# Winograd feed-forward kernel: Pool sums queued one product ahead, upper and lower halves of each operand queued apart, rows of odd tiles loaded later

## The chip, the cores and the metric

The kernel runs on one NeuronCore of a Trainium2 chip. Its engines are TensorE (PE in the profile, with its weight loads as PEld), VectorE (DVE), ScalarE (ACT), GpSimd (POOL) and SyncE (SP, which issues the DMAs). Each engine takes its instructions strictly in the order in which the program issued them; semaphores hold an instruction until what it reads is written and what it overwrites has been read. The metric is device time in microseconds of one execution, the median over runs.

## What is computed

One block of a transformer trunk on 1024 tokens of width 1024, all in float32: RMS norm, sliding-window attention with sinks, output projection, residual; then RMS norm, a SwiGLU feed-forward layer with inner width 2816, residual, and a last RMS norm.

```
h = rms_norm(x, norm_mix);  x = x + sliding_window_sink_attention(h, ...)
gu = rms_norm(x, norm_ffn) @ w_gate_up
x = x + (silu(gu[:, :2816]) * gu[:, 2816:]) @ w_down
out = rms_norm(x, final_norm)
```

## The kernel before, in words

**Precision.** Each float32 operand is split into an upper half (`hi`, a rounded copy in fp32r, written by ScalarE) and a lower half (`lo` = source minus upper half). A product is three matmuls: hi x hi, hi x lo, lo x hi. The `lo` of a gate-up weight is written by VectorE; in the down stage the `lo` of an activation is written by GpSimd and that of a weight by VectorE.

**Seven products for eight.** Both feed-forward matrix products are done in Winograd's form of Strassen's scheme: 2 x 2 blocks, seven products numbered 1 to 7. Some operands are sums or differences of blocks. GpSimd makes these ("sums"), and a summed operand can be split only after its sum.

**Gate-up stage** (lines 873 to 1092). 22 groups `g` of 256 columns, even ones gate, odd ones up. From group 2 on every group is seven products in the order 1, 6, 5, 7, 2, 4, 3, of 12 matmuls each. Products 1 and 2 accumulate in one PSUM bank (A), 6 and 7 in B, 5 and 3 in C, 4 alone in D. The second product of a bank may start only when VectorE has read the first: `u(0)` (line 1011) reads B between products 6 and 7, `c("C", 1, 1, 1)` (line 1015) reads C between 5 and 3. The weights are prepared by `prep` (line 888): optional sums (line 901), `hi` (line 921), `lo` (line 925). `prep_more` (line 936) is called ahead of every product and prepares, into nine slots, the operand for the product eight ahead as soon as the slot of the product just done is free (two operands in one call where slots come in pairs). After each odd group `act_sums` (line 979) makes four sums of the finished activations on GpSimd (line 989) and stores them to DRAM.

**Down stage** (lines 1137 to 1362). Four rounds of 2, 2, 2 and 3 pairs; per round seven products in the order 1, 2, 6, 7, 5, 3, 4; a product is four token columns `j` of 3 matmuls per pair (24 matmuls for 2 pairs, 36 for 3). Its operands sit in 16 slots: per product and pair one of activations ("s", loaded from DRAM) and one of down weights ("w"). `d_steps` (line 1178) gives the steps of an operand: for a weight operand of product 6 two sums (lines 1212 and 1216), of products 7 and 4 one sum (line 1212), then `hi` (line 1232) and `lo` (line 1235). Results leave PSUM at once: in round 0 products 1 and 7 are copied to `y1`, `y7` by ScalarE (line 1314), all others are added to `acc` by VectorE (line 1316). Products 1 and 2 share a bank per column, and so do 6 and 7, and 5 and 3: the second one's matmuls wait until the first one's result has been read. `acc` starts as the rows of the residual, eight DMAs (line 1279). Last come 16 products of four leftover chunks (line 1390) and the final norm.

**Order.** No scheduler reorders anything. A list `Q` holds steps with due times; every matmul of these stages issues one tick, and a tick issues what is due. So a due time decides only the place of a step in its engine's queue, not when it runs. `d_more` (line 1242) is called ahead of every down product and after the last seven gate-up products. Before the change it and `prep_more` strung the steps of an operand one right behind another:

```
for i, st in enumerate(steps):                                  # prep_more
    Q.put(1 + i * spread // len(steps), st)
for k, st in enumerate(st for steps in todo for st in steps):   # d_more
    Q.put(1 + k * spread // total, st)
```

## Time and profile before

| | |
|---|---|
| time, median of 3 runs | 1066.96 us (1066.46 to 1068.29) |
| the profiled execution's own time | 1066.94 us |
| its span, first to last instruction | 1065.1 us |
| granted TensorE clock, mean over the span | 0.979 of full speed |
| busy: PE, DVE, ACT, POOL | 1007.2, 617.8, 454.6, 573.4 us |

Times in the views are microseconds from the start of the span. In a timeline row the columns are start, duration, engine, line, operation, output <- inputs, count, and in brackets the idle time of the engine ahead of the row with what ended it. A matmul shown as 0.4 us long is pipelined: in these stages one starts every 0.233 us. "L1054" is line 1054.

### The profile page before, as it was taken

What the parts mean: (1) busy time and instruction counts of PE and PEld (TensorE: products, weight loads), DVE (VectorE), ACT (ScalarE), POOL (GpSimd) and SP (SyncE); (2) the same over time, 40 slices, a digit from 0 to 9 for tenths busy, and PEclk for the clock granted to TensorE, in tenths of its full rate; (3) what the DMA queues carried; (4) which work ended last, traced back from release to release, by engine and by line L of the source; (5) the groups of instructions that cost most, each with busy time, mean ns of one, the idle gap of its engine ahead of it and who ended that gap; (6) DMA issues with size and microseconds to landing.
All of it is one profiled execution on the core that took longest, in us unless ns stands there. A gap on an engine that the chain in (4) does not pass through costs nothing. (4 is left out here: it accounts for less than half of the span.)

```text
span 1065.1 us, 13843 instructions
## 1 busy us (share of the span) xinstructions
PE 1007.2 (95%) x4740; PEld 828.8 (78%) x4740; DVE 617.8 (58%) x1070; ACT 454.6 (43%) x955; POOL 573.4 (54%) x557
## 2 busy tenths in 40 slices
PE   7999999999986899999999999999998889898997
PEld 7888888888765698787888777778887768687885
DVE  5421778777975665554454554545543467564774
ACT  5432778777844542331332332322323533333334
POOL 4634655565424555375375374374336676667573
PEclk8999999999988999999999999999999899999999
DMA  8458556564437311342231340331336925242202
GB/s 269 132 131 204 151 144 158 145 195 136 140 99 213 124 60 60 129 148 75 75 129 39 129 145 23 129 128 42 129 119 206 351 94 188 89 139 76 92 40 119
DMA packets 98983, 138.28 MB, mean 130 GB/s; under 512 B 6368, under 2 KB 66784, under 8 KB 98912
## 3 DMA queue, kind: packets, MB, share of 16 engines
q1 hardware_dynamic: 98624, 136.61, 41.1%
q8 instruction: 37, 0.61, 0.2%
q10 hardware_dynamic: 288, 0.79, 0.2%
q14 instruction: 34, 0.28, 0.1%
HBM read 99.89 MB, written 35.39 MB: 127 GB/s over the span
## 5 line engine op out<-in xcount | busy, mean ns | idle before, releaser
L1305 PE MATMUL d<-HH 128*128 128x512 f32 x756 | 179.4, 400 | 17.9 <-DVE y L1316 8.1
L1305 PEld LDWEIGHTS d<-HH 128*128 128x128 f32 x756 | 146.1, 194 | 51.1 <-ACT HH L1232 13.1
L967 POOL TENSOR_TENSOR gate<-gate,up 128x512 f32<-128x512 f32 x33 | 47.2, 1430 | 177.5 <-issue 130.9
L925 DVE TENSOR_TENSOR ws<-sum,ws 128x512 fp32r<-128x512 f32 x88 | 81.2, 932 | 92.8 <-ACT ws L921 92.5
L1054 PE MATMUL gu_A<-HH,ws 128*128 128x512 f32 (+2 forms) x552 | 132.3, 388 | 0.0
L1235 POOL TENSOR_TENSOR HH<-raw_s,HH 128x512 fp32r<-128x512 f32 x63 | 90.8, 1456 | 74.9 <-ACT HH L1232 66.1
L251 PE MATMUL pc<-HH,wc_c 128*128 128x512 f32 x480 | 122.0, 398 | 0.0
L1054 PEld LDWEIGHTS gu_A<-HH,ws 128*128 128x128 f32 x552 | 101.7, 188 | 22.9
L921 ACT ACTIVATE ws<-sum 128x512 fp32r<-128x512 f32 x88 | 54.4, 627 | 141.3 <-POOL sum L901 108.3
L251 PEld LDWEIGHTS pc<-HH,wc_c 128*128 128x128 f32 x480 | 87.3, 188 | 17.9
L496 POOL TENSOR_SCALAR t<-t,st 128x256 f32<-128x256 f32 (+1 forms) x128 | 60.7, 494 | 52.2 <-DVE st L494 36.1
L921 ACT ACTIVATE ws<-raw_g 128x512 fp32r<-128x512 f32 x66 | 40.6, 626 | 100.2 <-issue 41.2
L1235 DVE TENSOR_TENSOR HH<-wd,HH 128x512 fp32r<-128x512 f32 x62 | 51.3, 831 | 50.9 <-ACT HH L1232 50.9
L925 DVE TENSOR_TENSOR ws<-raw_g,ws 128x512 fp32r<-128x512 f32 x66 | 65.5, 1002 | 23.6 <-ACT ws L921 22.9
L483 ACT ACTIVATE t<-t,st 128x256 f32<-128x256 f32 (+1 forms) x128 | 61.9, 485 | 26.6 <-DVE st L475 26.5
L1054 PE MATMUL gu_B<-HH,ws 128*128 128x512 f32 x264 | 67.0, 403 | 6.0 <-DVE u L1011 6.0
L1054 PE MATMUL gu_C<-HT,ws 128*128 128x512 f32 (+2 forms) x288 | 67.6, 382 | 0.6 <-DVE ws L925 0.6
L63 POOL TENSOR_TENSOR wc_c<-raw_c,wc_c 128x1024 fp32r<-128x1024 f32 x20 | 48.0, 2402 | 34.9 <-ACT wc_c L60 34.6
L1054 PE MATMUL gu_D<-HT,ws 128*128 128x512 f32 (+2 forms) x276 | 66.5, 388 | 0.0
L1054 PE MATMUL gu_C<-HH,ws 128*128 128x512 f32 x264 | 65.5, 397 | 0.9 <-DVE gate L1015 0.9
L1054 PE MATMUL gu_B<-HT,ws 128*128 128x512 f32 (+2 forms) x276 | 65.9, 387 | 0.0
L1054 PEld LDWEIGHTS gu_B<-HH,ws 128*128 128x128 f32 x264 | 50.5, 192 | 19.3 <-issue 7.3
(173 smaller groups left out, 1946.1 us busy)
## 6 DMA issues: line engine op xcount, KB each, us to landing
raw_g<-in_ffn_w_gate_up_dram SPq DMA_DIRECT2D x44, 512.0 KB, 4.1
raw_s<-actp SPq DMA_DIRECT2D x27, 512.0 KB, 3.4
wd<-in_ffn_w_down_dram SPq DMA_DIRECT2D x22, 512.0 KB, 4.1
raw_c<-in_swa_w_in_dram SPq DMA_DIRECT2D x20, 512.0 KB, 4.1
actp<-up SPq DMA_DIRECT2D x18, 512.0 KB, 5.4
qs<-qst SPq DMA_DIRECT2D x64, 128.0 KB, 2.5
qt<-qs SPq DMA_DIRECT2D x32, 256.0 KB, 4.4
actp<-gate SPq DMA_DIRECT2D x27, 256.0 KB, 4.5
```

What stands on the lines that cost most here:

```text
L63: lo_eng.tensor_tensor(lo, src, f(hi), ALU.subtract)
L251: nc.tensor.matmul(ps, wc[:, wl, k], hh[:, :, hl, k, :], start=(n == 0), stop=(n == 3 * NK - 1))
L483: nc.scalar.activation(self.tt[:, g, b0:], self.tt[:, g, b0:], AF.Exp, bias=st[:, 0, g : g + 1], scale=-1.0, accum_out=st[:, 3, g : g + 1],)
L496: nc.gpsimd.tensor_scalar(self.tt[:, g, b0:], self.tt[:, g, b0:], st[:, 2, g : g + 1], 0.0, ALU.mult, ALU.add)
L921: nc.scalar.activation(w[:, 0], src(), AF.Copy)
L925: nc.vector.tensor_tensor(w[:, 1], src(), f(w[:, 0]), ALU.subtract)
L967: nc.gpsimd.tensor_tensor(gate[:, s], gate[:, s], ups[kp, f_][:, s], ALU.mult)
L1054: nc.tensor.matmul(v4(ps)[:, j0:j1], w[:, wl, k], moving(i, hl, k, j0, j1), start=(first and part != "l" and n == 0), stop=(n == 11), skip ...
L1235: eng.tensor_tensor(dst[:, 1], v4(src()), f(dst[:, 0]), ALU.subtract)
L1305: nc.tensor.matmul(v4(ps), a_[:, a, j], d_[:, b], start=(first and n == 0), stop=(n == 3 * len(ps_) - 1), skip_group_check=True,)
```

## The change

In `prep_more` the sums of an operand come first, 3 ticks apart, then `hi` some `lag` ticks after the first sum and `lo` another `lag` ticks after `hi`; `lag` is 8, or 3 and 4 in the entry of the stage. The second operand of a call follows half a spread later instead of at the same time. The first call in the main loop comes 12 ticks earlier. `act_sums` spaces its four sums by 11 ticks instead of 5 and stores at tick 48 instead of 30.

In `d_more` the sums of weight operands are given out on their own, up to about one product ahead of the operands whose `hi` is due (`nsum` against `ndop`); an operand's `hi` is given out only in a call after its sum has been issued (`summed`), and its `lo` 10 ticks after its `hi`. `BEHIND` keeps a sum that overwrites a block behind the `lo` that still reads it. Calls after the last gate-up products take 3 operands instead of 2, and the queue is no longer emptied (`Q.flush()`) between the stages.

The `acc` tiles are laid out in the order 0, 2, 4, 6, 1, 3, 5, 7; the even rows are loaded at the start of the down stage, the odd ones at ticks 48, 64, 80 and 96 after it, the row of the final norm at tick 150.

```diff
--- before.py
+++ after.py
@@ -923,6 +923,7 @@
         def lo():
             w = ws[item]
             nc.vector.tensor_tensor(w[:, 1], src(), f(w[:, 0]), ALU.subtract)
+            ready.add(item)
             if i == 7:
                 Raw.done(lk)
             if i == 3:
@@ -930,17 +931,21 @@
 
         return steps + [hi, lo]
 
-    made = set()
+    made, ready = set(), set()
     nprep = 0
 
-    def prep_more(n, spread):
+    def prep_more(n, spread, lag=8):
         nonlocal nprep
+        base = 1
         while n and nprep < len(seq) and ws_free(nprep):
-            steps = prep(seq[nprep])
-            for i, st in enumerate(steps):
-                Q.put(1 + i * spread // len(steps), st)
+            *sums_, hi, lo = prep(seq[nprep])
+            for i, st in enumerate(sums_):
+                Q.put(base + 3 * i, st)
+            Q.put(base + (lag if sums_ else 0), hi)
+            Q.put(base + (lag if sums_ else 0) + lag, lo)
             nprep += 1
             n -= 1
+            base += spread // 2
 
     Q = Queue()
 
@@ -986,7 +991,7 @@
             (u0[:, a], u1[:, a], g0[:, a], ALU.subtract),
             (u1[:, b], g1[:, a], u0[:, a], ALU.subtract),
         )):
-            Q.put(2 + 5 * i, lambda dst=dst, x_=x_, y_=y_, op=op: nc.gpsimd.tensor_tensor(dst, x_, y_, op))
+            Q.put(2 + 11 * i, lambda dst=dst, x_=x_, y_=y_, op=op: nc.gpsimd.tensor_tensor(dst, x_, y_, op))
 
         def store():
             rows_ = actp_dram[kp]
@@ -996,7 +1001,7 @@
             nc.sync.dma_start(rows_[1], u0)
             nc.sync.dma_start(rows_[2], u1)
 
-        Q.put(30, store)
+        Q.put(48, store)
 
     def after(g, i):
 
@@ -1046,6 +1051,7 @@
         first = i not in (2, 7, 3)
         if first and part != "l":
             banks[g, letter] = pool.tile([P, 512], F32, tag=tag, name=f"gu_{g}_{letter}")
+        assert (g, i) in ready, (part, g, i, nprep, Q.now)
         ps, w = banks[g, letter], ws[g, i]
         j0, j1 = {"g": (0, 4), "h": (0, 3), "l": (3, 4)}[part]
         n = 0
@@ -1082,13 +1088,13 @@
                             W.want(j + 3)
                         o_mm(i, 2 * c2 + ci, nh, wt)
                 ob_done = j + 1
-                prep_more(2, 8)
+                prep_more(2, 8, 3)
         wts = [W.get(42), W.get(43)]
         for i in range(2):
             for nh in range(2):
                 for c in (6, 7):
                     o_mm(i, c, nh, wts[nh])
-            prep_more(2, 8)
+            prep_more(2, 8, 3)
         ob_done = 44
 
 
@@ -1239,45 +1245,76 @@
 
         return steps + [hi, lo]
 
-    def d_more(n, spread):
-        nonlocal ndop
-        todo = []
-        while n and ndop < len(dops):
+    nsum, d_ready = 0, set()
+
+    def d_more(n, span):
+
+
+        nonlocal ndop, nsum
+        his, tts = [], []
+        while n and len(his) < n and ndop < len(dops):
             o = ndop
             free = (NG - 1, (1, 7, 2, 3)[o // 4]) in done if o < 16 else dops[o - 16][1:] in d_done
-            steps = d_steps(dops[o]) if free else None
+            steps = d_steps(dops[o]) if free and (dops[o] not in summed or summed[dops[o]]) else None
             if steps is None:
                 break
-            todo.append(steps)
+            his.append((dops[o], steps[-2], steps[-1]))
             ndop += 1
-            n -= 1
-        total = sum(len(st) for st in todo)
-        for k, st in enumerate(st for steps in todo for st in steps):
-            Q.put(1 + k * spread // total, st)
+        while nsum < min(ndop + n + 1, len(dops)):
+            op = dops[nsum]
+            if op in summed:
+                steps = d_steps(op)
+                if steps is None or op[1] in BEHIND and ("w", BEHIND[op[1]], op[2]) not in d_ready:
+                    break
+
+                def last(op=op, st=steps[-3]):
+                    st()
+                    summed[op] = True
+
+                tts += [*steps[:-3], last]
+            nsum += 1
+        for k, st in enumerate(tts):
+            Q.put(2 + k * span // len(tts), st)
+        for k, (op, hi, lo) in enumerate(his):
+
+            def low(op=op, lo=lo):
+                lo()
+                d_ready.add(op)
+
+            Q.put(1 + k * span // len(his), hi)
+            Q.put(11 + k * span // len(his), low)
+
+    BEHIND = {6: 1, 4: 2}
+    summed = {op: False for op in dops if op[0] == "w" and op[1] in (6, 7, 4)}
 
     o_products()
     for n, item in enumerate(head):
-        if Q.now >= 96 + 48:
-            prep_more(2, 11)
+        if Q.now >= 96 + 36:
+            prep_more(2, 11, 4 if n < 8 else 8)
         product(*item)
         if item[0] != "h":
             done.add(item[1:])
             after(*item[1:])
         if len(head) - 1 - n < 7:
             w_more()
-            d_more(2, 10)
-    Q.flush()
+            d_more(3, 11)
     ht_cm.__exit__(None, None, None)
 
 
     accp = ctx.enter_context(tc.tile_pool(name="accp", bufs=1, reuse_waits="tile"))
-    acc = [accp.tile([P, D], F32, name=f"acc_{t}") for t in range(NT)]
+    acc = {t: accp.tile([P, D], F32, name=f"acc_{t}") for t in (0, 2, 4, 6, 1, 3, 5, 7)}
     y1 = [accp.tile([P, 512], F32, name=f"y1_{j}") for j in range(4)]
     y7 = [accp.tile([P, 512], F32, name=f"y7_{j}") for j in range(4)]
     wbc = row("wbc_fin", "wbc")
-    for t in (0, 2, 4, 6, 1, 3, 5, 7):
+
+    def load_acc(t):
         nc.sync.dma_start(acc[t], x2_dram[t])
-    nc.sync.dma_start(wbc, norm_fin.partition_broadcast(P))
+
+    for t in (0, 2, 4, 6):
+        load_acc(t)
+    for t in (1, 3, 5, 7):
+        Q.put(40 + 8 * t, lambda t=t: load_acc(t))
+    Q.put(150, lambda: nc.sync.dma_start(wbc, norm_fin.partition_broadcast(P)))
 
 
     def d_out(i, j):
@@ -1300,6 +1337,7 @@
             ps = dbanks[bank, j]
             n = 0
             for p in ps_:
+                assert {("s", i, p), ("w", i, p)} <= d_ready
                 a_, d_ = d_slot["s", i, p], d_slot["w", i, p]
                 for a, b in ((0, 0), (0, 1), (1, 0)):
                     nc.tensor.matmul(
@@ -1355,7 +1393,7 @@
     for r, ps_ in enumerate(drounds):
         for i in DORDER:
             w_more()
-            d_more(2 * len(ps_) + 1, 12 * len(ps_) - 3)
+            d_more(2 * len(ps_) + 1, 12 * len(ps_))
             d_product(r, i)
             for p in ps_:
                 d_done.add((i, p))
@@ -1372,12 +1410,10 @@
     for j in range(4):
         for k, st in enumerate(y_sums(j)):
             Q.put(6 + 22 * j + 5 * k, st)
-    while ndop < len(dops):
+    while len(d_ready) < len(dops):
         w_more()
-        before = ndop
         d_more(16, 4)
         Q.tick()
-        assert ndop > before
     for t in range(NT):
         for nh in range(2):
             pool, tag = (psg, "g") if nh else (psa, "a")
```

## Rows read from the trace of the kernel before

**Rows 1.** The page, busy time of each engine over the span.
```profile
PE 1007.2 (95%) x4740; PEld 828.8 (78%) x4740; DVE 617.8 (58%) x1070; ACT 454.6 (43%) x955; POOL 573.4 (54%) x557
```

**Rows 2.** The waits of TensorE: waited for, us in total, times, longest.
```profile
PE d L1305 <- DVE y L1316: 8.1, 2, 4.0
PE d L1305 <- ACT y L1314: 6.4, 1, 6.4
PE gu_B L1054 <- DVE u L1011: 6.0, 3, 2.1
...
PE d L1305 <- DVE acc L1316: 3.4, 2, 3.2
```

**Rows 3.** The timeline of TensorE, gate-up stage from group 2 on.
```profile
415.14 2.96 PE L1054 MATMUL gu_A<-HH,ws 128*128 128x512 f32 x12
417.94 2.96 PE L1054 MATMUL gu_B<-HT,ws 128*128 128x512 f32 x12
...
499.35 2.96 PE L1054 MATMUL gu_C<-HT,ws 128*128 128x512 f32 x12
504.40 4.58 PE L1054 MATMUL gu_B<-HH,ws 128*128 128x512 f32 x12 [2.09 <-DVE u L1011]
508.81 2.96 PE L1054 MATMUL gu_A<-HH,ws 128*128 128x512 f32 x12
...
666.52 3.04 PE L1054 MATMUL gu_B<-HH,ws 128*128 128x512 f32 x12 [2.08 <-DVE u L1011]
...
707.83 3.04 PE L1054 MATMUL gu_B<-HH,ws 128*128 128x512 f32 x12 [1.87 <-DVE u L1011]
```

**Rows 4.** The timeline of all engines, group 6 (it starts at 493.75).
```profile
497.62 1.30 POOL L901 TENSOR_TENSOR sum<-raw_g,raw_g 128x512 f32<-128x512 f32 x1
...
499.61 1.11 DVE L925 TENSOR_TENSOR ws<-sum,ws 128x512 fp32r<-128x512 f32 x1 [4.74 <-ACT ws L921]
500.12 1.74 POOL L901 TENSOR_TENSOR sum<-sum,raw_g 128x512 f32<-128x512 f32 x1
...
502.56 1.08 DVE L925 TENSOR_TENSOR ws<-sum,ws 128x512 fp32r<-128x512 f32 x1 [1.85 <-ACT ws L921]
...
503.57 0.68 DVE L1011 TENSOR_TENSOR u<-gu_B,p 128x512 f32<-128x512 f32 x1
```

**Rows 5.** The timeline of TensorE, down stage and the leftover products.
```profile
817.10 5.61 PE L1305 MATMUL d<-HH 128*128 128x512 f32 x24
829.10 23.84 PE L1305 MATMUL d<-HH 128*128 128x512 f32 x96 [6.39 <-ACT y L1314]
...
873.98 39.91 PE L1305 MATMUL d<-HH 128*128 128x512 f32 x168 [4.04 <-DVE y L1316]
917.92 58.98 PE L1305 MATMUL d<-HH 128*128 128x512 f32 x252 [4.03 <-DVE y L1316]
980.12 34.30 PE L1305 MATMUL d<-HH 128*128 128x512 f32 x144 [3.22 <-DVE acc L1316]
1014.25 43.68 PE L1390 MATMUL dl<-HH 128*128 128x512 f32 x192
```

**Rows 6.** The groups by line, 817 to 1014 us: busy, mean ns | idle before, releasers.
```profile
L1235 POOL TENSOR_TENSOR HH<-raw_s,HH 128x512 fp32r<-128x512 f32 x58 | 83.7, 1458 | 53.1 <-ACT HH L1232 44.3 <-PE d L1305 7.4 <-issue 1.3
...
L1235 DVE TENSOR_TENSOR HH<-wd,HH 128x512 fp32r<-128x512 f32 x55 | 45.3, 823 | 43.3 <-ACT HH L1232 43.3
...
L1232 ACT ACTIVATE HH<-wd 128x512 fp32r<-128x512 f32 x58 | 35.8, 622 | 52.6 <-POOL wd L1212 47.6 <-PE d L1305 4.9
```

**Rows 7.** The timeline of all engines around the start of the down stage.
```profile
810.88 1.76 POOL L967 TENSOR_TENSOR gate<-gate,up 128x512 f32<-128x512 f32 x1
...
827.94 0.63 ACT L1232 ACTIVATE HH<-wd 128x512 fp32r<-128x512 f32 x1 [2.97 <-POOL wd L1212]
828.47 0.58 ACT L1314 ACTIVATE y<-d 128x512 f32<-128x512 f32 x1
```

**Rows 8.** The DMA issues, 780 to 880 us: KB each, median us to landing.
```profile
acc<-x2s SPq DMA_DIRECT2D x8, 512.0 KB, 7.3
```

## The prediction

> **What bounds the kernel now.** I read the busy times first: TensorE is busy 95% of the span, the next engine 58% [rows 1]. So a gain can only come from its idle time. Next, its waits: 17.9 us in the down stage (8.1 + 6.4 + 3.4), most of the rest of what this change can reach behind `u` in the gate-up stage [rows 2]. Then its timeline, to put these waits into places and to see what they cost beyond the idle time itself.
>
> Gate-up: a product starts 2.80 us after the one before it (415.14 to 417.94) [rows 3], so a tick is 2.80 / 12 = 0.233 us. From 415.14 to the first down product at 817.10 [rows 3, 5] there are 20 groups of 7 products: 140 x 2.80 = 392.0 us at full pace, 401.96 in the trace, so **9.96 us are lost**. Most of it sits at three like places, where the second product of bank B waits for `u(0)`: 2.09, 2.08 and 1.87 us. The first also costs clock: that product needs 4.41 us (504.40 to 508.81) instead of 2.80 [rows 3].
>
> Down: 756 matmuls at a tick each are 176.4 us; from 817.10 to 1014.25 [rows 5] it takes 197.15. So **20.75 us are lost**: 17.9 of waiting [rows 2], the rest slower matmuls behind the waits (the 96 from 829.10 show 23.84 us instead of 22.4) [rows 5].
>
> Why TensorE waits is read in the other engines. In group 6 VectorE starts a `lo` at 502.56 that has waited 1.85 us for ScalarE's `hi`, which waited for a sum; the sums stand on GpSimd in turns with the four of `act_sums`. Only behind this `lo` comes `u(0)`, at 503.57, though product 6 was through long before, and product 7, due at 499.35 + 2.80 = 502.15, starts at 504.40 [rows 3, 4]. The down stage has the same chain in nearly every weight operand of products 6, 7 and 4: ScalarE idles 47.6 us ahead of `hi` for a sum, VectorE 43.3 us ahead of `lo` for a `hi`, GpSimd 44.3 us ahead of its own `lo` for a `hi` that stands behind the stalled one [rows 6]. The three engines run one after the other, and the result reads that TensorE needs queue behind them. Nobody lacks throughput.
>
> **The change part by part.** No instruction is added or removed; all of it is order. So every term is waiting.
>
> *Gate-up, sums and `act_sums`.* By the new due times, in a group like 6, GpSimd's order is multiplication, first `act_sums` step, first weight sum, second weight sum, and only then the second `act_sums` step (tick 21 instead of 15). Up to the first weight sum this is the old order, so I take its row: done at 498.92. `hi` follows (0.63), then the same `lo` as before, 499.61 to 500.72 [rows 4]. The other operand's `lo` falls due at tick 29, behind `u(0)` at 28. `u(0)` can then run from 500.72 to 501.40, 0.75 us before 502.15: the wait goes. The fourth wait (ahead of product 3, from the same mixing one product later) goes alike: its sum at tick 37 stands ahead of the last `act_sums` step, not behind all four. Everywhere else `lo` is due 8 ticks (1.9 us) behind `hi` and ahead of `u(0)` only where the sum was given out 16 ticks before. What is late next: weight operands are ready 22 ticks after their call at the latest, and are used eight products (96 ticks) after it; the store of `act_sums` moves by 18 ticks (4.2 us), and its tiles are next written 84 ticks (19.6 us) after it; the raw tiles freed by a later `lo` refill two groups ahead. I cost these at nothing. Bounds for the stage: 0 to 9.96 us gained, and a loss as in the third rival; I take 9.96, since the place with the least room keeps 0.75 us.
>
> *Down, sums ahead and `lo` 10 ticks behind `hi`.* Following the due times call by call, each operand's `lo` is issued at least 19 ticks (4.4 us) ahead of the product that reads it (tightest in the last round, product 6 and 7), and each sum a call ahead of its `hi`. GpSimd has 58 `lo` at 1.458 us [rows 6] and by the code 36 sums; at 1.30 [rows 4] that is 84.6 + 46.8 = 131 us of the 176. Its fullest stretch is the start of the last round: 15 steps in 80 ticks (18.7 us), 20.5 us of work, and the `hi` concerned come over 20 ticks after their sums. VectorE then waits for nothing of GpSimd's, and results are read within the 15 ticks (3.5 us) that the order gives them. A raw tile is refilled over 50 ticks (11.7 us) before its `hi`. Bounds: 0 to 20.75 us gained; I take all but the boundary, below.
>
> *Boundary of the stages.* Here ScalarE copies `y` only behind a `hi` that waited 2.97 us for its sum: 6.39 us of TensorE's idle time [rows 5, 7]. In the new order that `hi` (product 7, second pair) stands ahead of the copies too, and its sum is the fifth GpSimd step after the multiplication that ends at 812.64 [rows 7]: two sums, a `lo`, two sums. At 1.30, 1.458 or 1.74 us each [rows 4, 6] it ends at 819.1, 819.9 or 821.3; three `hi` and a copy (2.3 us) [rows 7] later the first `y` is out, at 821.4, 822.2 or 823.6. Product 2 is due at 817.10 + 24 x 0.233 = 822.7. So 0 to 0.9 us are left, and I take 0.5.
>
> *Odd rows later, no flush.* SP now issues four loads, not nine, ahead of the raw tiles. Even rows go out behind a store that needs a multiplication on GpSimd ending near 822.5; with 7.3 us to landing [rows 8] they are there at 829.8, four adds end by 832.5, and product 7 first needs VectorE at 833.9: hidden, by 1.4 us. The last odd tile is loaded at tick 96 and added to at tick 123, 6.3 us later, so VectorE may wait 1 us; product 3 needs that column only 15 ticks (3.5 us) on. Nothing, then; if the loads took 3 us longer, some 2 us would show once.
>
> *Entry* (lags of 3 and 4, first call 12 ticks earlier): one wait under a microsecond may go; counted at nothing.
>
> **Sum**, against the profiled execution's own 1066.94 us (the median is 1066.96, the same): 1066.94 - 9.96 - 20.75 + 0.5 = **1036.7 us**. What lies outside the two stages is untouched.
>
> **A rule that speaks against it.** A sum takes 1.30 us when VectorE is idle and 1.74 beside a `lo`, which itself takes 1.11 [rows 4]. The Trainium skill, GPSIMD Engine Reference, section 1. Specifications, says that GpSimd shares its SBUF interfaces with VectorE and contends with instructions of two SBUF inputs; by that rule, the trace agrees, sums no longer followed by a waiting VectorE would all run at the long time. It is the first rival.
>
> **The rivals.**
> 1. *GpSimd stretched by VectorE.* With every step at 1.74 us [rows 4] the first weight sum of a group like 6 ends 1.3 us later, `u(0)` ends at 502.7 and product 7 loses 0.75 us with the hand-over, three times 0.75 = 2.3; the boundary keeps 0.9 instead of 0.5. In the down stage 94 steps x 1.74 = 164 us, still under 176. Result 1039.4. For: both long and short times are in the trace. Against: VectorE is busy 58% [rows 1], and mean 1.458 [rows 6] already holds much overlap. Chance 0.16.
> 2. *The boundary keeps its wait.* GpSimd still works off the last multiplications and four sums while ScalarE's copies stand behind a `hi`. If something ahead (a late down weight, a `lo`) pushes that chain by 6 us, the old 6.39 us [rows 5] stay: 1036.7 + 5.9 = 1042.6. For: it is the only place where my room is under 1 us and several queues meet. Chance 0.13.
> 3. *`u(0)` is late in every group: slower.* The new order puts a `lo` at ticks 17 to 26 ahead of `u(0)` in all 20 groups. If that `lo` begins to wait beyond about 6.6 us into the group (product 7 is due at 8.40; `lo`, `u(0)` and hand-over need 1.8), every group loses what group 6 lost, 504.40 - 502.15 = 2.25 us [rows 3]: 1036.7 + 45.0 = 1081.7. For: the fixed place in the queue. Against: in the rows the first sum is done 5.2 us into the group even behind two other steps [rows 4]. Chance 0.03.
> 4. *It does not do what it says:* the sums still run late, because GpSimd reaches them no sooner, and the waits move instead of going: 1066 us. Against: GpSimd idles 44.3 us of the down stage for others [rows 6]. Chance 0.03.
> 5. *Only the down stage gains*, because another read takes the place of `u(0)`: 1036.7 + 9.96 = 1046.7. Chance 0.05.
>
> **How the numbers follow.** Forecast 1036.7 with chance 0.60; its own range, the boundary and the entry, is 1035 to 1039. The range takes in rivals 1 and 2: its low end is 1066.94 - 30.71 less about 1 us for the entry and the spread of runs, 1035.0; its high end 1042.6 and the runs' spread of 1.3, 1044.0. It leaves out rivals 3 to 5, 0.11 of the chance, and some room for what I missed. A measurement of this kernel tells about 0.2% (2.1 us) from no change. Faster by more: 0.60 + 0.16 + 0.13 + 0.05 = 0.94; within: 0.03 (rival 4); slower: 0.03 (rival 3).
>
> **What would show it.** Right: TensorE's waits for `u` at line 1011 and for `y` and `acc` at line 1316 are gone; the down stage takes 176 to 178 us and groups 2 to 21 take 392; ScalarE's wait for sums at lines 1212 and 1216 and VectorE's for `hi` fall from over 40 us to a few; the clock stays full through both stages. Wrong: a wait of several us behind the copies to `y` at the start of the down stage (rival 2); `u` waits in many groups (rival 3); mean times of GpSimd's sums near 1.7 with short waits left (rival 1); new waits of TensorE for an operand's `lo`, which would mean that the operands came too late after all.

## The result and the profile after

| | before | changed |
|---|---|---|
| time, median of 4 runs each | 1067.62 us (1066.46 to 1069.64) | 1038.68 us (1037.09 to 1040.88) |
| the profiled execution's own time | 1066.94 us | 1039.65 us |
| its span | 1065.1 us | 1037.9 us |
| granted TensorE clock, mean over the span | 0.979 | 0.983 |

The ratio is 0.973, with a 95% interval of 0.970 to 0.975: 2.7% faster. The forecast was 1036.7 us in a range of 1035 to 1044. The profiled execution of the changed kernel lies 1 us above its median, so the working below is against 1039.65.

The page of the changed kernel, busy time of each engine (it answers to [rows 1]): TensorE's busy time fell by 6.4 us, GpSimd's rose by 15.5 and VectorE's by 25.3 at the same number of instructions.

```profile
PE 1000.8 (96%) x4740; PEld 826.4 (80%) x4740; DVE 643.1 (62%) x1070; ACT 454.8 (44%) x955; POOL 588.9 (57%) x557
```

The waits of TensorE in the changed kernel, from 400 us on (they answer to [rows 2]; waited for, us in total, times, longest). Of some 24 us in [rows 2], 5 are left, and the larger of the two is a wait that the kernel before did not have in this place: `acc`, once, 4.1 us, ahead of product 7 of the first round.

```profile
PE d L1343 <- DVE acc L1354: 4.1, 1, 4.1
PE gu_B L1060 <- DVE u L1016: 0.9, 1, 0.9
```

The timeline of TensorE in the changed kernel (it answers to [rows 3, 5]).

```profile
415.45 2.96 PE L1060 MATMUL gu_A<-HH,ws 128*128 128x512 f32 x12
...
738.51 3.06 PE L1060 MATMUL gu_B<-HH,ws 128*128 128x512 f32 x12 [0.90 <-DVE u L1016]
...
808.62 16.74 PE L1343 MATMUL d<-HH 128*128 128x512 f32 x72
829.42 158.06 PE L1343 MATMUL d<-HH 128*128 128x512 f32 x684 [4.07 <-DVE acc L1354]
987.32 43.70 PE L1426 MATMUL dl<-HH 128*128 128x512 f32 x192
```

Two numbers are read from this view for every kernel below. **A** is the gate-up stage, from the start of group 2 to the first down product: 808.62 - 415.45 = 393.17 us (401.96 before [rows 3, 5]). **B** is the down stage, from its first product to the first leftover product: 987.32 - 808.62 = 178.70 us (197.15 before [rows 5]). They account for the result: 8.79 + 18.45 = 27.24 of the 27.29 us between the two profiled executions. What lies ahead of group 2 differs between kernels that are the same there (its start lies between 412.2 and 415.6 us in all runs), so the whole times of single runs tell little below 2 us, and A and B are compared. A repeats to a few hundredths in kernels with the same gate-up part and no change at its end; B lies between 176.15 and 178.70 us in the five kernels below that have the changed down part as it is (changed, e2, e7, e8, e11), so a difference in B of 2.5 us tells nothing.

The groups by line in the changed kernel, 808.62 to 987.3 us (they answer to [rows 6]): VectorE's idle time ahead of the `lo` of weights went from 43.3 to 5.0 us, ScalarE's for a sum from 47.6 to 2.5. But one GpSimd sum now takes 1584 ns, and one VectorE `lo` 1098 instead of 823.

```profile
L1241 POOL TENSOR_TENSOR HH<-raw_s,HH 128x512 fp32r<-128x512 f32 x60 | 88.0, 1484 | 22.5 <-ACT HH L1238 22.5
L1241 DVE TENSOR_TENSOR HH<-wd,HH 128x512 fp32r<-128x512 f32 x54 | 59.2, 1098 | 5.0 <-ACT HH L1238 5.0
...
L1238 ACT ACTIVATE HH<-wd 128x512 fp32r<-128x512 f32 x58 | 35.5, 619 | 7.8 <-PE d L1343 4.9 <-POOL wd L1218 2.5
L1218 POOL TENSOR_TENSOR wd<-wd 128x512 f32<-128x512 f32 x10 | 15.8, 1584 | 3.4 <-DVE HH L1241 3.4
```

The timeline of all engines in the changed kernel, around the start of the down stage (it answers to [rows 7]). The first copies of `y` run at 813.51 and wait for nothing. What is late is the residual: SP issues the even rows at 815.74, the first add waits for them until 822.46, the add at 827.46 for the last one, and TensorE, which stopped at 829.42 - 4.07 = 825.35, goes on behind the next add. The two single `acc` rows at 825.04 and 827.39 are the first two odd ones.

```profile
813.51 1.55 ACT L1352 ACTIVATE y<-d 128x512 f32<-128x512 f32 x3
814.88 0.33 SPq L978 DMA_DIRECT2D act<-gate  x1
815.74 2.29 SPq L1311 DMA_DIRECT2D acc<-x2s  x4
822.46 0.69 DVE L1354 TENSOR_TENSOR acc<-d,acc 128x512 f32<-128x512 f32 x1 [7.05 <-DMA acc<-x2s]
...
825.04 0.43 SPq L1311 DMA_DIRECT2D acc<-x2s  x1
...
827.39 0.43 SPq L1311 DMA_DIRECT2D acc<-x2s  x1
827.46 0.69 DVE L1354 TENSOR_TENSOR acc<-d,acc 128x512 f32<-128x512 f32 x1 [0.55 <-DMA acc<-x2s]
```

Windows of the changed kernel (us, then PE, PEld, DVE, ACT and POOL busy with their counts, granted clock, DMA share, GB/s). The wait is paid twice: 4.07 us of idling, and then 35 matmuls in 10.58 us at a granted clock of 0.72, while the DMA engines run at their full share.

```profile
825.42:829.42 4.00, 0.00 (x1) 0.00 (x1) 2.65 (x5) 0.26 (x1) 4.00 (x4) 0.88 1.02 408
829.42:840.00 10.58, 10.58 (x35) 8.49 (x36) 4.92 (x8) 5.45 (x10) 3.35 (x4) 0.72 1.03 413
840.00:860.00 20.00, 20.00 (x90) 16.57 (x89) 16.55 (x22) 8.19 (x16) 18.90 (x14) 1.00 0.43 152
```

### The profile page after: what moved, and what is told of

It reads as the page before. It is cut to its first block, busy times and chain, and to the rows that moved or that the text cites. A ratio compares the mean times of both kernels' runs of the same rounds, so it can differ in the third digit from the quotient of the medians.

```text
span 1037.9 us, 13830 instructions
## 1 busy us (share of the span) xinstructions
PE 1000.8 (96%) x4740; PEld 826.4 (80%) x4740; DVE 643.1 (62%) x1070; ACT 454.8 (44%) x955; POOL 588.9 (57%) x557
## 4 chain that ended last, share of the span: by engine, by line
PE 63%; DMA 1%; POOL 1%; DVE 1%; ACT 0%; issue 0%; SPq 0%; POOLq 0%; DVEq 0%; ACTq 0%
PE d L1343 16%; PE gu_A L1060 12%; PE gu_B L1060 12%; PE gu_C L1060 12%; PE gu_D L1060 6%; PE dl L1426 4%; DMA acc<-x2s 1%; PE mo L1073 1%; DVE ws L925 0%; POOL sum L901 0%; POOL wc_oB L63 0%; POOL xr L641 0%; PE pt_b L620 0%; SPq L1311 0%; ACT wc_oB L60 0%
## 5 line engine op out<-in xcount | busy, mean ns | idle before, releaser
L1343 PE MATMUL d<-HH 128*128 128x512 f32 x756 | 174.8, 394 | 4.1 <-DVE acc L1354 4.1
L1343 PEld LDWEIGHTS d<-HH 128*128 128x128 f32 x756 | 143.7, 190 | 35.0 <-DVE acc L1354 4.5
L972 POOL TENSOR_TENSOR gate<-gate,up 128x512 f32<-128x512 f32 x33 | 50.4, 1529 | 162.5 <-issue 71.5
L251 PEld LDWEIGHTS pc<-HH,wc_c 128*128 128x128 f32 x480 | 87.3, 188 | 17.9
L925 DVE TENSOR_TENSOR ws<-raw_g,ws 128x512 fp32r<-128x512 f32 x66 | 71.4, 1090 | 35.7 <-ACT ws L921 35.4
L1238 ACT ACTIVATE HH<-raw_s 128x512 fp32r<-128x512 f32 x63 | 39.4, 625 | 85.0 <-PE d L1343 36.7
L1241 DVE TENSOR_TENSOR HH<-wd,HH 128x512 fp32r<-128x512 f32 x62 | 66.4, 1076 | 12.5 <-ACT HH L1238 12.5
L1354 DVE TENSOR_TENSOR acc<-d,acc 128x512 f32<-128x512 f32 x80 | 54.3, 686 | 31.5 <-PE d L1343 21.1
```

Of the source, the lines that this page charges most:

```text
L251: nc.tensor.matmul(ps, wc[:, wl, k], hh[:, :, hl, k, :], start=(n == 0), stop=(n == 3 * NK - 1))
L925: nc.vector.tensor_tensor(w[:, 1], src(), f(w[:, 0]), ALU.subtract)
L972: nc.gpsimd.tensor_tensor(gate[:, s], gate[:, s], ups[kp, f_][:, s], ALU.mult)
L1241: eng.tensor_tensor(dst[:, 1], v4(src()), f(dst[:, 0]), ALU.subtract)
L1343: nc.tensor.matmul(v4(ps), a_[:, a, j], d_[:, b], start=(first and n == 0), stop=(n == 3 * len(ps_) - 1), skip_group_check=True,)
L1354: nc.vector.tensor_tensor(dst, ps, dst, ALU.add)
```

## The experiments

Three open questions: whether the two stages' gains are separate; which of the new spacings carries each; and what the boundary costs. All twelve kernels against the two of the change, A and B as above (times are of one run, except where a range stands):

| kernel | time, us | A, us | B, us |
|---|---|---|---|
| before | 1066.94 | 401.96 | 197.15 |
| changed | 1039.65 | 393.17 | 178.70 |
| e1_gate_only | 1058.34 | 393.16 | 197.62 |
| e2_down_only | 1046.79 | 400.42 | 178.17 |
| e3_lo_close | 1047.17 | 399.20 | 181.64 |
| e4_sums_inline | 1038.18 | 393.16 | 179.42 |
| e5_act_late | 1039.28 | 393.16 | 179.99 |
| e6_rows_at_once | 1036.71 | 393.17 | 177.60 |
| e7_act_sums_old | 1036.70 | 393.78 | 178.41 |
| e8_prep_old | 1040.32 | 395.38 | 176.15 |
| e9_inline_close | 1067.82 | 399.41 | 200.67 |
| e10_odd_copied | 1031.36 (1030.32 to 1032.91, 5 runs) | 393.14 | 171.62 |
| e11_changed_again | 1038.89 (1037.92 to 1041.83, 4 runs) | 393.17 | 177.55 |
| e12_odd_only | 1039.62 | 393.16 | 178.78 |

The kernel before gave 1064.76 to 1067.93 us beside them.

### Each stage alone

e1 is the kernel before with the new `prep_more` and `act_sums`; e2 is the changed kernel with the old ones.

The edit of e1 is the part of the change's diff above `d_steps`, and the calls of `prep_more` (without the assertions). The edit of e2 takes the same part back, save for the lag in two calls, where it is no longer used; these are lines of it:

```diff
...
-            Q.put(base + (lag if sums_ else 0), hi)
-            Q.put(base + (lag if sums_ else 0) + lag, lo)
+            steps = prep(seq[nprep])
+            for i, st in enumerate(steps):
+                Q.put(1 + i * spread // len(steps), st)
...
-            Q.put(2 + 11 * i, lambda dst=dst, x_=x_, y_=y_, op=op: nc.gpsimd.tensor_tensor(dst, x_, y_, op))
+            Q.put(2 + 5 * i, lambda dst=dst, x_=x_, y_=y_, op=op: nc.gpsimd.tensor_tensor(dst, x_, y_, op))
...
-        Q.put(48, store)
+        Q.put(30, store)
...
-        if Q.now >= 96 + 36:
-            prep_more(2, 11, 4 if n < 8 else 8)
+        if Q.now >= 96 + 48:
+            prep_more(2, 11)
```

> Only the gate-up part of the change (prep_more, act_sums, the earlier first call); the down stage as before. My theory, that each part removes its own waits: groups 2 to 21 take about 393 us instead of 402, the down stage stays at about 197, time about 1058. Rival, that TensorE only arrives earlier at the down stage and gives the gain back there waiting for sums or DMAs: the down stage grows to 203 or more, time 1064 or more.

> Only the down part (sums ahead, lo 10 ticks behind hi, odd rows later, no flush); prep_more and act_sums as before. My theory: groups 2 to 21 take 402 us again, the down stage about 179 with the wait of about 4 us ahead of product 7, time about 1048. Rival, that this wait comes from the faster gate-up stage: the wait is gone, the down stage takes about 172, time about 1041.

The waits of TensorE in e1, from 400 us on: those of the down stage as before, `u` down from 6.0 to 0.9.

```profile
PE d L1309 <- DVE y L1320: 8.1, 2, 4.0
PE d L1309 <- ACT y L1318: 6.4, 1, 6.4
...
PE gu_B L1058 <- DVE u L1015: 0.9, 1, 0.9
```

e1 has the A of the changed kernel and the B of the one before, e2 nearly the other way round. Its A of 400.42 is 1.54 us under before, all of it in one product of group 6 (4.41 us before, 2.87 in e2; see the last section), and its B still has the wait for `acc`, of 4.08 us. Both theories hold: the two gains are separate and they add. So what the down stage gained owes nothing to the gate-up stage's order.

### The gate-up stage: which spacing

e2 in two pieces: e7 takes only the old spacing of `act_sums` back (the two middle hunks of the diff above), e8 only the old `prep_more` with its calls (the first and the last).

> The changed kernel with the four sums behind each odd group 5 ticks apart and their store at tick 30, as before the change. Theory, that the order on GpSimd (weight sums between those four) is what took the waits for u away: they come back in some groups, groups 2 to 21 take 397 us or more, time 1042 or more. Rival, that the distance between upper and lower half did it, as in the down stage: groups 2 to 21 stay under 394.5, time within 2 us of 1038.7.

> The changed kernel with the old prep_more (sums, upper and lower half strung together, late first call) but the four sums behind each odd group 11 ticks apart. Theory, that the order on GpSimd is enough: waits for u gone, groups 2 to 21 take under 395, time under 1041. Rival, that the distance between upper and lower half is needed: two or more waits for u of about 2 us, groups 2 to 21 take 397 or more, time 1042 or more.

A is 393.78 in e7 and 395.38 in e8. Of the 7.25 us between e2 and the changed kernel the new `prep_more` alone brings 6.64 and the new spacing of `act_sums` alone 5.04. So the theory of e7, that the order on GpSimd alone took the waits away, fell, and its rival came out; in e8 A lies just above the theory's 395, and neither the theory nor the rival came out. The timeline of TensorE in e8 at group 6, the place of [rows 4], shows the wait of 2.09 us down to 0.94 (two more waits, of 0.98 and 0.74, are left in e8):

```profile
503.49 3.04 PE L1056 MATMUL gu_B<-HH,ws 128*128 128x512 f32 x12 [0.94 <-DVE u L1012]
```

So the prediction's picture holds: `u(0)` was late by a `lo` that waited for a weight sum, which stood behind other steps on GpSimd. To take away either the mixing or the `lo` that waits brings most of the gain, and only both bring all.

The 0.9 us that are left, in group 18, are in every kernel with the new `prep_more`. The timeline of all engines of the changed kernel there:

```profile
732.76 1.69 DVE L925 TENSOR_TENSOR ws<-raw_g,ws 128x512 fp32r<-128x512 f32 x1 [2.83 <-ACT ws L921]
...
734.38 3.48 DVE L925 TENSOR_TENSOR ws<-sum,ws 128x512 fp32r<-128x512 f32 x2
735.57 1.74 POOL L901 TENSOR_TENSOR sum<-raw_g 128x512 f32<-128x512 f32 x1
...
737.78 0.68 DVE L1016 TENSOR_TENSOR u<-gu_B,p 128x512 f32<-128x512 f32 x1
```

Three `lo` stand ahead of `u(0)` and each takes 1.7 us beside GpSimd's steps, 5.1 us in a row. This is the third rival's place (a `lo` ahead of `u(0)`), in one group of 20 and at 0.9 us. Taking it away was not tried.

### The down stage: which spacing

e3 puts `lo` one tick behind its `hi` again and keeps the sums ahead. e4 keeps `lo` ten ticks behind and gives the sums out with their operand, in the tick of `hi` and right ahead of it. e9 does both.

The edit of e3:

```diff
-            Q.put(11 + k * span // len(his), low)
+            Q.put(2 + k * span // len(his), low)
```

The edit of e4 (the loop over `nsum` and the condition on `summed` go):

```diff
-            his.append((dops[o], steps[-2], steps[-1]))
+            his.append((dops[o], steps))
...
-        for k, (op, hi, lo) in enumerate(his):
+        for k, (op, steps) in enumerate(his):
+            *sums_, hi, lo = steps
...
+            for st in sums_:
+                Q.put(1 + k * span // len(his), st)
```

> The changed kernel with the lower half of every down operand given out one tick behind its upper half instead of ten. Theory, that the sums given out ahead carry the gain of the down stage: it stays within 2 us of 178.7, time 1037 to 1041. Rival, that the distance between upper and lower half carries it: VectorE waits for ScalarE again by 20 us or more, the down stage takes 190 or more, time 1050 or more.

> The changed kernel with the sums of down weights given out right ahead of their upper half, no longer a product ahead; the lower half still ten ticks behind. Theory, that the sums given out ahead carry the gain: ScalarE waits for sums by 40 us or more, TensorE waits for results again, the down stage takes 190 or more, time 1050 or more. Rival, that the distance of the lower half alone is enough: the down stage stays under 183, time under 1043.

> The changed kernel with both spacings of the down stage undone: sums right ahead of their upper half, lower half one tick behind it (gate-up part, row order and missing flush kept). Theory after the runs so far, that either spacing alone keeps VectorE from standing behind a sum, so that the old loss comes back only when both are gone: TensorE waits for results several times again, the down stage takes 190 to 200, time 1050 to 1062. Rival, that the missing flush or the order of the rows carries the gain: the down stage stays under 184.

The theories of e3 and e4 both fell, and so did e3's rival (B is 181.64, neither within 2 us of 178.7 nor 190). e4, without the sums ahead, keeps nearly all: B is 179.42, as its rival had it. The waits of ScalarE and VectorE in e4 from 809 to 987 us (the stage without its first 2.6 us) show how:

```profile
ACT HH L1238 <- POOL wd L1218: 23.8, 13, 3.0
ACT HH L1238 <- POOL t L1222: 18.5, 8, 3.6
...
DVE HH L1241 <- ACT HH L1238: 7.3, 6, 3.0
```

ScalarE waits 42 us for sums again, but VectorE only 7.3 for a `hi`, and it is VectorE's queue that holds the reads of PSUM. e9 is the test of that. The same view of e9:

```profile
ACT HH L1238 <- POOL wd L1218: 46.5, 18, 3.4
...
DVE HH L1241 <- ACT HH L1238: 72.5, 29, 5.1
```

VectorE waited 73.2 us for a `hi` in the kernel before:

```profile
DVE HH L1235 <- ACT HH L1232: 73.2, 29, 3.9
```

TensorE's timeline in e9:

```profile
826.00 25.66 PE L1331 MATMUL d<-HH 128*128 128x512 f32 x102 [6.92 <-DVE up L1020]
...
875.04 39.95 PE L1331 MATMUL d<-HH 128*128 128x512 f32 x168 [4.48 <-DVE y L1342]
919.01 59.01 PE L1331 MATMUL d<-HH 128*128 128x512 f32 x252 [4.03 <-DVE y L1342]
981.24 34.41 PE L1331 MATMUL d<-HH 128*128 128x512 f32 x144 [3.22 <-DVE acc L1342]
```

B is 200.67: with both spacings gone the old loss is back, and from 875 us on TensorE has the waits of [rows 5] again, 4.48, 4.03 and 3.22 us. So within the stage neither half of the change is needed by itself; either is nearly enough, and with both missing it runs as before. Only its start differs: there TensorE waits 6.92 us for `up`, in the place where e3 loses time, instead of 6.39 for `y`. With this, and with an A of 399.41 like that of e3, B and the time came out above the ranges of the theory, 200 and 1062. The rival is out: the missing flush and the order of the rows do not carry the gain. What they are worth by themselves (and the third operand in the last gate-up calls, and the new order of the `acc` tiles) was not tried.

At the boundary the sums ahead do count. TensorE's timeline in e4 has there the wait of [rows 5] again, for ScalarE's copy of `y` behind a `hi` that waits for its sum:

```profile
806.42 5.61 PE L1331 MATMUL d<-HH 128*128 128x512 f32 x24
817.71 168.29 PE L1331 MATMUL d<-HH 128*128 128x512 f32 x732 [5.68 <-ACT y L1340]
```

It takes the place of the 4.07 us for `acc`, so the sum hardly moves. So ScalarE's waiting did cost TensorE here, at the one place where ScalarE's queue holds the read that TensorE needs.

e3 loses 6 us ahead of the down stage and 3 at its start, in a place of its own; behind that it has no wait, so in the steady state the sums ahead are enough. The timeline of all engines in e3, at the last gate-up products: a `hi` waits 4.45 us for a down weight's DMA, its `lo`, right behind it, holds VectorE, and `u(0)` stands behind that; TensorE waits 3.14 us, and two more waits (3.68 and 2.47) follow.

```profile
797.20 0.63 ACT L1238 ACTIVATE HH<-wd 128x512 fp32r<-128x512 f32 x1 [4.45 <-DMA wd<-in_ffn_w_down_dram]
797.86 0.69 DVE L1241 TENSOR_TENSOR HH<-wd,HH 128x512 fp32r<-128x512 f32 x1 [4.70 <-ACT HH L1238]
798.47 0.68 DVE L1016 TENSOR_TENSOR u<-gu_B,p 128x512 f32<-128x512 f32 x1
```

### The boundary: what makes the rows late

The changed kernel issues the even rows behind the store of a gate tile (L978), which waits for GpSimd's multiplication. e5 moves the stores of the last group to tick 60, behind the even rows. e6 loads all eight rows at the start, as before the change. e10 moves the stores to tick 140 and takes the odd rows out of the first 30 us: the first results of odd tiles are copied into `acc`, and the rows come into tiles of their own (issued between 877 and 894 us, 70 us or more into the stage) and are added from 907 to 945 us, in the third and fourth round and not in round 1, as its expectation has it (8 more adds on VectorE); the row of the final norm moves to tick 290. e11 is the changed kernel once more, on the chip of e10. e12 is e10 without the moved stores.

The edit of e5, and with 140 in the place of 60 one part of e10:

```diff
-                nc.sync.dma_start(act_dram[2 * kp + f_], gate)
+                store = lambda: nc.sync.dma_start(act_dram[2 * kp + f_], gate)
+                if g == NG - 1:
+                    Q.put(60, store)
+                else:
+                    store()
```

The edit of e6:

```diff
-    for t in (0, 2, 4, 6):
+    for t in (0, 2, 4, 6, 1, 3, 5, 7):
         load_acc(t)
-    for t in (1, 3, 5, 7):
-        Q.put(40 + 8 * t, lambda t=t: load_acc(t))
-    Q.put(150, lambda: nc.sync.dma_start(wbc, norm_fin.partition_broadcast(P)))
+    nc.sync.dma_start(wbc, norm_fin.partition_broadcast(P))
```

The edit of e12, and the other part of e10:

```diff
...
-        Q.put(40 + 8 * t, lambda t=t: load_acc(t))
...
+        Q.put(300 + 12 * t, lambda t=t: load_odd(t))
+        for nh in range(2):
+            Q.put(420 + 24 * t + 24 * nh, lambda t=t, nh=nh: add_odd(t, nh))
...
+                elif r == 0 and i in (5, 4):
+                    nc.vector.tensor_copy(dst, ps)
```

> The changed kernel with the two stores of the last gate and up pair issued 60 ticks later, so that SP reaches the four even residual rows before it would wait for GpSimd's last multiplications. Theory, that these rows come late because they are issued late (behind a store that waits for GpSimd): they are issued about 5 us earlier, TensorE's wait of 4.1 us ahead of product 7 goes, and with it the slow clock behind it: time about 1032. Rival, that they come late because the DMA engines are full at over 400 GB/s: they still land after 825, the wait stays within 1.5 us of 4.1, time 1036 to 1040.

> The changed kernel with all eight residual rows and the row of the final norm loaded at the start of the down stage again (even ones first). Theory, that the odd rows loaded later keep the DMA engines free for the raw activations and down weights: the even rows land no later than now, but raw activations land 5 us or more later and TensorE waits a few us more, time 1040 to 1046. Rival, that this part of the change is worth nothing: time 1036 to 1040.

e5 issues the even rows at 809.13, and the wait for them is gone, as the theory had it: 126 matmuls run through. But B is 179.99, and the time that the theory gave, 1032, did not come. TensorE's timeline in e5:

```profile
836.23 1.67 PE L1347 MATMUL d<-HH 128*128 128x512 f32 x6 [0.30 <-DVE acc L1358]
840.00 1.66 PE L1347 MATMUL d<-HH 128*128 128x512 f32 x6 [2.10 <-DVE acc L1358]
845.13 141.99 PE L1347 MATMUL d<-HH 128*128 128x512 f32 x618 [3.47 <-DVE acc L1358]
```

The odd rows are late in their place. SP's timeline in e5 shows one reason: the second of them, due at 64 x 0.227 = 14.5 us into the stage (821.5), is issued at 827.31, behind a load of a raw tile that waits for a GpSimd `lo` (by SP's waits 24.5 us in all between 805 and 846, 6.2 the longest). It is not e5's own moved stores that hold it up there: the changed kernel, which has none between these rows, issues the same row at 827.39.

```profile
826.94 0.32 SPq L776 DMA_DIRECT2D raw_s<-actp  x1
827.31 0.43 SPq L1315 DMA_DIRECT2D acc<-x2s  x1
...
834.12 0.32 SPq L1315 DMA_DIRECT2D acc<-x2s  x1
```

e6 has a wait of 2.92 us and B 177.60; the changed kernel run twice gives 178.70 and 177.55. So the theory of e6 fell, and what loading the odd rows later is worth cannot be told from nothing.

> The changed kernel with 3 MB taken out of the first 30 us of the down stage: the first results of odd tiles are copied instead of added, their residual rows are loaded in round 1 and added then (8 more additions on VectorE), and the last two activation stores go out 140 ticks later. Theory, that the wait ahead of product 7 is a matter of bytes in that stretch (over 400 GB/s): it goes and does not come back elsewhere, the down stage takes 171.5 to 174, time 1031 to 1034, 0.4 to 0.7% below the changed kernel. Rival, that the wait moves once more (raw activations, weights, or VectorE busy with the additions): down stage 176 or more, time 1036 to 1040.

> The changed kernel itself, on the same chip as the version above, to compare the two: 1037 to 1041.

TensorE's timeline in e10: the 756 matmuls of the down stage run without a gap.

```profile
806.53 171.78 PE L1359 MATMUL d<-HH 128*128 128x512 f32 x756
978.15 43.70 PE L1444 MATMUL dl<-HH 128*128 128x512 f32 x192
```

B is 171.62, and the whole 1031.36 us, 0.967 of before (95% interval 0.966 to 0.968), 7.5 us under the changed kernel beside it: the version that beats both. (e11, the changed kernel, has a ratio of 0.974 there, 0.973 to 0.976.) It differs from the changed kernel in two things, so the last run asks which of them counts.

> The odd tiles' copies as in the run before this one, but the stores of the last group's gates stay where the changed kernel has them, ahead of the even rows. Theory (taking the odd tiles' 2 MB of rows out of the first 30 us is enough by itself): no TensorE wait in the down stage, B 171.5 to 173.5 us, time 1030 to 1034 us. Rival (the stores ahead of the even rows still make these late, and both moves are needed): a wait of 1 to 4 us ahead of the tenth or so product of the down stage stays, B 175 us or more, time 1034 to 1040 us.

The theory fell. TensorE's timeline in e12:

```profile
808.52 16.67 PE L1355 MATMUL d<-HH 128*128 128x512 f32 x72
830.50 156.97 PE L1355 MATMUL d<-HH 128*128 128x512 f32 x684 [5.31 <-DVE acc L1368]
```

The even rows are issued at 815.60, as in the changed kernel, and are late by as much. The odd rows were no part of this wait: the changed kernel issues the first of them only at 825.04. So two waits lie one behind the other: the even rows' (removed by e5 alone, kept by e12) and the odd rows' (uncovered by e5). Each removed alone gains nothing, both together gain 7 us. So the even rows are late by when they are issued (in e5, 6.6 us sooner, they are there in time), and not by the odd rows' bytes, although e10 came out in the range of its theory. How much of the odd rows' lateness in e5 is SP's queue and how much the bytes (8 us from 832 on move 413 GB/s there, the two moved stores among them) was not taken apart; e10 moves the stores further than e5 does, and its stores with the odd rows of the changed kernel were not tried.

## Why the prediction was right, and where it was not

**Right: all of it is order, and the loss is TensorE's waiting.** Two whole rows of [rows 2], the waits for `y`, are gone, `u` is 0.9 instead of 6.0, and nothing was gained elsewhere: A and B hold 27.24 of 27.29 us. Of the signs that were named for it, VectorE's and ScalarE's waits fell as said (5.0 and 2.5 us left); `acc` did not go, B is 178.70 and not 176 to 178, and the clock did not stay full. That the two stages are separate terms of a sum is shown by e1 and e2.

**Gate-up: forecast 392.0, measured 393.17.** Of the difference 0.9 us is the wait in group 18, which the step "everywhere else `lo` is due 8 ticks behind `hi`" passed over; the rest, some 0.3 us, is spread over 140 products.

**Down: forecast 176.9, measured 178.70, by two errors that nearly cancel.** That the two lie so close is luck. With the floor right the same working gives 1036.7 - 4.8 = 1031.9, the time of e10 and not that of the changed kernel. The first error is the floor, "756 matmuls at a tick each are 176.4 us". The tick was taken from the gate-up stage (0.2333 us). The down stage's own pace is 171.62 / 756 = 0.2270 us, seen in e10 with no wait in it; so the floor is 171.6 and the kernel before lost 25.5 us, not 20.75: 17.9 of waiting and 7.6 of slower matmuls. A row for this pace was at hand: the leftover products, 192 in 43.68 us, are 0.2275 us each [rows 5]. The row of 252 in 58.98, which comes to 0.2340 each [rows 5], starts behind a wait of 4 us and holds slower matmuls. The second error is the step that comes next.

**The step that failed: "Odd rows later, no flush", costed at nothing, "hidden, by 1.4 us".** Put on the new axis (the stage starts 8.48 us earlier) it had the store's multiplication end at 814.0, the rows there at 821.3, the four adds done at 824.0 and product 7 in need of VectorE at 825.4. Measured: 814.9, the first add at 822.46, the last row only at 827.4, and TensorE stopping at 825.35. So the need was right and the landing wrong. One number was taken for all rows, the median of eight transfers in the kernel before, 7.3 us [rows 8], counted from the end of the multiplication. Of the 6.1 us by which the last row is later than that, 0.9 are the multiplication's. Another 3.1 go until SP has issued the store, a weight and the four rows, one after the other (814.9 to 818.0), which the step left out. The last 2.1 are the landing: the last row lands 827.4 - 818.0 = 9.4 us after the last issue, while the DMA engines are at a share of 1.02 (816 to 824 us). In the kernel before the slowest of the eight took 10.0 us. The price is 178.70 - 171.62 = 7.1 us, 4.07 of idling and 3 of slower matmuls behind it, where the step itself had allowed 2 for loads that are late by 3. Also, as e5 shows, behind this wait stood another one, for the odd rows, that the step called nothing too.

**The boundary's `y`: right.** First copy out at 822.2 forecast on the old axis, 813.7 on the new; measured, three copies run from 813.51 to 815.06, so the first is out near 814. e4 shows that the sums ahead did it.

**Too strong: that the sums ahead free the down stage.** The prediction gave the gain to the chain sum, `hi`, `lo` as a whole. e4 and e3 show that in the steady state it is enough to cut it at one place, and e4 that ScalarE may wait 42 us for sums as long as VectorE does not: TensorE waits for it only at the start of the stage, 5.68 us.

**The rivals.** The second named the right place and the wrong wait: not `y` behind a `hi`, but `acc` behind a DMA, and the time stayed under its 1042.6. The first came true in its premise, in good part: a sum now takes 1.58 us and VectorE's `lo` 1.10 on average, where [rows 6] has 0.82 for the `lo` and the same view of the kernel before has 1.285 for the sum:

```profile
L1212 POOL TENSOR_TENSOR wd<-wd 128x512 f32<-128x512 f32 x11 | 14.1, 1285 | 0.0
```

In e9, where the waits are back, they take 1.36 and 0.89. The Trainium skill (GPSIMD Engine Reference, section 1. Specifications) says that GpSimd shares its SBUF interfaces with VectorE and contends with VectorE's instructions of two SBUF inputs; the trace agrees: both engines' steps are longer, by 0.30 and 0.28 us, where they wait less for each other. It cost TensorE nothing in the down stage: in e10 the `lo` of GpSimd takes 1581 ns and TensorE waits for none. The 0.9 us in group 18 are the exception. The fourth and fifth are out (the time fell, and A gained 8.79 us), and the third shows in one group of 20.

The entry of the gate-up stage, counted at nothing, can't be told: group 2 starts at 415.58 in e8 and 414.95 in e2, which have the old one, and between 412.20 and 415.45 in kernels with the new one.

## What to carry to other kernels

Where an engine takes its work strictly in order, look at what stands in the queue ahead of the read that TensorE needs: with some 73 us of VectorE waiting (before and e9) TensorE had three gaps of 3 to 4.5 us inside the stage, with 42 us of ScalarE waiting (e4) none there, and one, of 5.7 us, where ScalarE itself does the read. Cut the chain where that queue is. When all terms of a sum are waits, list for each place the next thing that is late, with the landing time of the last of a burst of transfers, not the median; here two late things one behind the other made each remedy alone look worthless. Take a stage's full pace from that stage, behind no wait.

## What the runs showed that was not expected

- The same matmul form runs at 0.2270 us in the down stage and 0.2333 in the gate-up stage (in the changed kernel 1561 in 364.10 busy us from 442 to 807 us), both at a granted clock of 1.00. Why stays open.
- A wait of 2.08 us costs clock in one run and not in another: at the same place of group 6 the product behind it takes 4.58 us in the kernel before [rows 3] and 3.03 in e2, at granted clocks of 0.61 and 1.00 until the next product starts. Why stays open.
- GpSimd's and VectorE's operations of the same shape stretch each other, 1.29 to 1.58 us and 0.82 to 1.10 us on average, as soon as they no longer wait for each other; a faster order lengthened its own steps, in the down stage at no cost to TensorE.
